# Nine more feed-forward slices as seven block products, with four single PSUM banks beside the attention's own

## The chip, the cores and the metric

The kernel runs on one core of a Trainium2 chip. The metric is the device time of one execution in microseconds (us). A run of the kernel before is a handful of executions; their median is given, and one more execution is recorded by the hardware profiler. Instructions are named by engine: PE is TensorE (matmuls), PEld its weight loads, DVE VectorE, ACT ScalarE, POOL GpSimd, SP SyncE, which issues most of the DMAs. L554 is line 554 of the kernel before.

## The reference, cut to what matters

One inference step of a two-layer decoder for 1024 prompt tokens and 8 sample tokens, which share all weights. Each layer is a mixer (layer 0: a gated linear recurrence and cross-attention into a memory; layer 1: stick-breaking attention over a shared key/value set, for the samples with pages of an old cache, and again cross-attention), and then a feed-forward network (FFN). D_MODEL is 1024, D_FF is 2816, all in float32. The change is in the FFN:

```python
def swiglu(h, w_gu, w_down):
    gate, up = jnp.split(h @ w_gu, 2, axis=-1)
    return (jax.nn.silu(gate) * up) @ w_down
...
    for l in range(DEPTH):
        ...
        h = h + rmsnorm(mix, g[1])
        h = h + rmsnorm(swiglu(rmsnorm(h, g[2]), w_gu[l], w_down[l]), g[3])
```

## The kernel before

**Tiling.** The activations lie with features on the 128 partitions and tokens on the free axis. The tokens form two groups: group 0 has 512 prompt tokens, group 1 has the other 512 and the 8 samples, 520 in all, always handled as two halves of 260 columns. To keep float32 accuracy, every operand is split into a high and a low part (`split_w` L253 for weights, `split_to` L283 for activations: a copy on ACT that rounds, a subtraction on DVE), and each product is three matmuls: high by high, high by low, low by high.

**The FFN.** The 22 slices of 128 hidden features are done in five parts of 5, 5, 4, 4 and 4 slices (`PARTS`, L615). In a part, each slice forms gate and up, their SwiGLU product is split into a tile of its own ("mid"), and then the part's down-projection (8 output blocks) adds to the result `R`. The plain form of a slice in group 1 takes 2 (gate, up) x 8 (blocks of 128 inputs) x 3 (split) x 2 (halves) = 96 matmuls of 260 columns.

**The block form.** `gate_up_w` (L526) treats a slice as a 2 x 2 block product, gate and up by upper and lower half of the inputs, times upper and lower half by the two halves of the tokens, and forms it from seven block products (Strassen, in Winograd's order): 7 x 4 x 3 = 84 matmuls. It needs four sums of weight blocks, which `weight_sums` (L590) makes ahead of time in DRAM by DMAs from DRAM to DRAM, half of them accumulating, all issued from POOL; and four sums of activation blocks for each pair of input blocks, which `sums_w` (L329) makes on DVE and ACT and puts into tiles `YT`. The products are gathered in four PSUM banks `Q(0)` to `Q(3)` (pa, pb, pc, pd at L559), with copies on ACT from one bank to the next (L561, L564) and additions on DVE (L572 to L578). Before the change only layer 1 of group 1, the last stage, uses it: `ffn_w` (L617) has 4 plain slices (`gate_up_q`, L501), in whose shade the activation sums are made, and then 18 in block form.

**PSUM.** PSUM has eight banks. Up to the last stage four of them are two double tiles `mmp`, one `mm` tile for each projection (`proj`, L269), three are single tiles `S()` for attention, transposes and the like, and one is `NS()`. For the last stage all are closed (L1439), and a pool `quads` of four tags with two buffers each takes their place; `S()` and `NS()` then take turns in two of its tags.

**Order of the work.** The program is written as generators. `weave` (L235) draws steps from several of them in given proportions; the framework's scheduler then orders each engine's instructions at compile time from that, and adds the waits. Each engine runs its own instructions in that fixed order. The stages around the change, in order (L1386 to L1443): layer 0's mixer for both groups and the FFN of group 0; then the shared keys and values of group 0; then (L1419) group 0's layer-1 attention together with parts 0 and 1 of group 1's layer-0 FFN; then (L1420) its parts 2, 3 and 4; group 1's keys and values; then (L1432) group 1's layer-1 attention and the samples' together with group 0's layer-1 FFN; and last (L1441 to L1443) group 1's layer-1 FFN in block form.

**Marks.** A step of `weight_sums` issues one DMA. So that it isn't issued too early, ACT copies one column of a recent result (`after()`) to a small tile, POOL copies that one (L605, the mark), and the DMA is queued behind the mark on POOL. The 40 steps of layer 1's sums lie in the stages of L1419 (16) and L1420 (24). POOL also issues the indirect loads of the old cache's pages (`page_loader`, L957), which the samples' attention uses in the stage of L1432: DVE multiplies a page tile (L923 for keys, L935 for values) that lies in one of the four buffers of `cpool`.

Of the kernel before, what the change touches and what calls it, by code (L numbers as in the profile page):

```python
# [9 lines left out]
F32 = mybir.dt.float32  # L10
# [8 lines left out]
P = 128  # L19
# [4 lines left out]
def tile_decoder(  # L24
# [22 lines left out]

    def pool(name, bufs, **kw):
        return ctx.enter_context(tc.tile_pool(name=name, bufs=bufs, **kw))
# [12 lines left out]
    cpool = pool("cpool", 4)  # L62
    banks = ctx.enter_context(ExitStack())
# [5 lines left out]
    uid = [0]  # L69

    def nm(s):
        uid[0] += 1
        return f"{s}_{uid[0]}"
# [10 lines left out]
    turn = [0]  # L84

# [3 lines left out]
    def NS():  # L89
        if single:  # L90
            return S()
        return nsp.tile([P, 512], F32, tag="ns", name=nm("ns"))
# [21 lines left out]
    def S():  # L114
        if single:
            turn[0] += 1
            return Q(3 * (turn[0] % 2))
# [211 lines left out]
    def sums_w(xs, ops):  # L329
# [4 lines left out]
        for k in range(4):  # L334
# [4 lines left out]
            o = (k % 2) * h  # L339

# [6 lines left out]
            for d, p, a, b in (  # L347
# [5 lines left out]
            ops.append([  # L353
                x0[:, :, :h], x1[:, :, :h], x1[:, :, h:n], z[:, :, o : o + h], u[:, :, o : o + h],
                y[:, :, :h], y[:, :, h : 2 * h],
            ])
            yield

    def YT():
        return xpool.tile([P, 2, NG[1]], F32R, tag="x0", name=nm("y"))  # L360
# [140 lines left out]
    def gate_up_q(l, f, xt):  # L501
# [3 lines left out]
        for j in range(2):  # L505
            w = split_w(w_gu[l], 0, ND, j * DFF + f * P)
            pp = [Q(2 * j + a) for a in range(2)]
            for k in range(ND):
                wh, wl = w[k]
                for wi, (wt, xi) in enumerate(((wh, 0), (wh, 1), (wl, 0))):  # L510
                    for a in range(2):
                        nc.tensor.matmul(  # L512
                            pp[a][:, :h], wt, xt[k][:, xi, a * h : (a + 1) * h],
                            start=(k == 0 and wi == 0), stop=(k == ND - 1 and wi == 2),
                        )
            for a in range(2):
# [3 lines left out]
                else:  # L520
                    last = nc.vector.tensor_mul(d, d, pp[a][:, :h])
        mt = M(F32R)
        split_to((mt[:, 0, :n], mt[:, 1, :n]), sg[:, :n])
        return mt, last

    def gate_up_w(l, f, ops, spl, raws):  # L526
# [53 lines left out]
        split_to((mt[:, 0, :n], mt[:, 1, :n]), sg[:, :n])  # L580
        return mt

    sums = {}
# [6 lines left out]
    def weight_sums(l, parts, after):  # L590

        for i in parts:
# [6 lines left out]
            for d, a, add in (  # L599
# [3 lines left out]
                tok = small([P, 1], tag="rr")  # L603
                nc.scalar.copy(tok, after())
                mark = nc.gpsimd.tensor_copy(small([P, 1], tag="mk", bufs=1), tok)  # L605
# [11 lines left out]
    class ffn_w:  # L617


        def __init__(self, l, x, plain):  # L620
            self.g, self.l, self.x, self.ops, self.plain, self.n, self.r, self.pi = 1, l, x, [], plain, 0, 0, 0
            self.R = self.acc = None
# [853 lines left out]
```

## Time and profile before

| | us |
|---|---|
| median of 3 runs | 2540.22 |
| lowest and highest of them | 2537.18, 2541.53 |
| the profiled execution | 2539.07 |
| its span, first to last instruction | 2537.4 |
| PE busy | 2503.8 |
| DVE busy | 1594.9 |
| ACT busy | 1220.6 |

The span is what the profile's views divide up; the profiled execution took 1.67 us more than its span. Busy times are unions of an engine's instructions; PE's ends are modelled, so that a full PE is better read from how many matmuls it finishes in a stretch. In a group's row stand line, engine, operation, the tile written and those read, the shapes, the count, then busy time and the mean of one in ns, and last the idle time of the engine just before these instructions and who ended it. In a view by windows each engine has its busy time and, in brackets, its number of instructions.

### The profile page before, as it was taken

The page shows a single profiled execution, that of the slowest core. Times are in us where ns is not written, and L with a number is a line of the kernel's source. Part 1 is how long each engine was busy: PE and PEld are TensorE (multiplying, and loading weights), DVE is VectorE, ACT ScalarE, POOL GpSimd, SP SyncE. Part 2 cuts the span into 40 slices and gives each one's busy share as a digit, 9 for nine tenths or more (in the row PEclk, how much of TensorE's full clock was granted, in tenths as well). Part 3 has the DMA queues.
Part 4 walks back from the last instruction along what each step waited for, and adds up shares of the span by engine and source line. Part 5 has one row for each costly group of instructions (what it writes and reads, how often), then busy time and mean ns, then how long its engine had stood idle before and what let it go on. Part 6 is the DMA issues. An engine that isn't in the chain of part 4 may idle for free. (4 is left out here: it accounts for less than half of the span.)

```text
span 2537.4 us, 40627 instructions
## 1 busy us (share of the span) xinstructions
PE 2503.8 (99%) x15437; PEld 2168.8 (85%) x15437; DVE 1594.9 (63%) x2860; ACT 1220.6 (48%) x2342; POOL 95.6 (4%) x139
## 2 busy tenths in 40 slices
PE   8999999999999999999999999999999999999998
PEld 6888888877877888989999989876676797999997
DVE  6666556655765576656544585776678638855665
ACT  6346543233434454555433454554455445554444
POOL 1000000000000000011111100012000000000000
PEclk9999999999999999999999999999999999999999
DMA  6352242234644446576678876544343333364542
GB/s 185 111 163 67 71 154 80 63 105 119 180 124 133 128 148 186 151 185 168 166 193 214 244 186 191 152 145 119 111 142 117 97 117 121 122 188 144 150 138 68
DMA packets 502221, 358.20 MB, mean 141 GB/s; under 512 B 19077, under 2 KB 451794, under 8 KB 502026
## 3 DMA queue, kind: packets, MB, share of 16 engines
q1 hardware_dynamic: 483466, 301.08, 39.8%
q0 software_dynamic: 18560, 54.53, 9.0%
q8 instruction: 121, 1.98, 0.3%
q14 instruction: 74, 0.61, 0.1%
HBM read 325.73 MB, written 75.94 MB: 158 GB/s over the span
## 5 line engine op out<-in xcount | busy, mean ns | idle before, releaser
L277 PE MATMUL mm<-x,ws 128*128 128x260 f32 (+1 forms) x7968 | 1425.2, 335 | 0.8 <-ACT x L401 0.8
L277 PEld LDWEIGHTS mm<-x,ws 128*128 128x128 f32 x7968 | 1190.5, 188 | 175.0 <-issue 28.5
L263 ACT CAST ws<-w 128x512 fp32r<-128x512 f32 x728 | 430.4, 592 | 724.7 <-PE mm L277 590.5
L264 DVE TENSOR_TENSOR ws<-w,ws 128x512 fp32r<-128x512 f32 x728 | 474.1, 654 | 301.2 <-ACT ws L263 290.7
L277 PE MATMUL mm<-m,ws 128*128 128x512 f32 (+1 forms) x2112 | 415.2, 347 | 0.0
L277 PEld LDWEIGHTS mm<-m,ws 128*128 128x128 f32 x2112 | 327.3, 189 | 53.5 <-issue 7.1
L669 PE MATMUL q<-m,ws 128*128 128x260 f32 x1056 | 128.8, 283 | 0.0
L669 PEld LDWEIGHTS q<-m,ws 128*128 128x128 f32 x1056 | 127.2, 188 | 0.4 <-ACT hT L487 0.2
L545 DVE TENSOR_TENSOR ws<-w,ws 128x512 fp32r<-128x512 f32 x126 | 86.4, 691 | 60.1 <-ACT ws L544 55.3
L554 PE MATMUL q<-y,ws 128*128 128x260 f32 x864 | 112.9, 283 | 0.0
L544 ACT CAST ws<-w 128x512 fp32r<-128x512 f32 x126 | 77.9, 621 | 69.0 <-PE q L669 26.1
L554 PEld LDWEIGHTS q<-y,ws 128*128 128x128 f32 x864 | 107.6, 188 | 0.0
L449 DVE TENSOR_TENSOR r<-r,mm 128x512 f32<-128x512 f32 (+1 forms) x96 | 66.1, 688 | 65.0 <-PE mm L277 64.1
L294 DVE TENSOR_SCALAR t<-mm 128x512 f32<-128x512 f32 (+1 forms) x82 | 56.8, 692 | 72.2 <-PE mm L277 71.2
L705 DVE TENSOR_TENSOR t<-t,mm 128x512 f32<-128x512 f32 (+1 forms) x66 | 45.6, 690 | 87.7 <-PE mm L277 87.7
L554 PE MATMUL q<-x,ws 128*128 128x260 f32 x648 | 86.3, 282 | 0.0
L298 DVE TENSOR_TENSOR t<-t,t 128x512 f32<-128x512 f32 (+1 forms) x66 | 45.8, 693 | 60.3 <-ACT t L297 60.2
L554 PEld LDWEIGHTS q<-x,ws 128*128 128x128 f32 x648 | 81.3, 188 | 0.0
L317 DVE TENSOR_TENSOR st<-st,n 128x512 f32<-128x512 f32 (+1 forms) x98 | 67.1, 692 | 6.7 <-ACT n L316 5.0
L285 DVE TENSOR_TENSOR m<-t,m 128x512 fp32r<-128x512 f32 (+1 forms) x88 | 61.1, 694 | 2.8 <-ACT m L284 1.4
L284 ACT CAST m<-t 128x512 fp32r<-128x512 f32 (+1 forms) x88 | 54.8, 623 | 11.7 <-DVE t L705 2.4
L964 POOL DMA_INDIRECT c<-in_cache_sb_k,pidx x16 | 16.4, 1025 | 1015.4 <-DVE x L285 796.7
(337 smaller groups left out, 2556.6 us busy)
## 6 DMA issues: line engine op xcount, KB each, us to landing
w<-in_w_gu SPq DMA_DIRECT2D x334, 256.0 KB
w<-in_w_down SPq DMA_DIRECT2D x160, 256.0 KB
w<-in_w_in_a SPq DMA_DIRECT2D x80, 256.0 KB
wsum<-in_w_gu POOLq DMA_DIRECT2D x18, 1024.0 KB, 9.2
w<-wsum SPq DMA_DIRECT2D x72, 256.0 KB
w<-in_w_o SPq DMA_DIRECT2D x64, 256.0 KB
wsum<-in_w_gu POOLq DMA_DIRECT2D x12, 1280.0 KB, 10.8
w<-in_w_mem_kv SPq DMA_DIRECT2D x32, 256.0 KB
```

The costliest lines, as they stand in the source:

```text
L263: nc.scalar.copy(ws[:, 0, :n, :], raw[:, :n, :])
L264: nc.vector.tensor_sub(ws[:, 1, :n, :], raw[:, :n, :], ws[:, 0, :n, :].bitcast(F32))
L277: nc.tensor.matmul(ps[:, a, : PW[g]], wt, xt[k][:, xi, o : o + PW[g]], start=(k == 0 and wi == 0), stop=(k == nk - 1 and wi == 2),)
L284: nc.scalar.copy(dst[0], src)
L285: nc.vector.tensor_sub(dst[1], src, dst[0].bitcast(F32))
L294: nc.vector.tensor_scalar(sv(x, g), pv(ps, g), -44.0, None, op0=ALU.max)
L317: nc.vector.tensor_add(acc[:, :n], acc[:, :n], t[:, :n])
L449: nc.vector.tensor_add(dst, dst, pv(ps, g))
L544: nc.scalar.copy(w[:, 0, :], src)
L545: nc.vector.tensor_sub(w[:, 1, :], src, w[:, 0, :].bitcast(F32))
L554: nc.tensor.matmul(ps[:, :h], w[:, wj, k * P : (k + 1) * P], x[:, xi, :], start=(first and k == 0 and wi == 0), stop=(k == 3 and wi == 2), ...
L669: nc.tensor.matmul(pp[a][:, :h], wt, mids[k][:, xi, a * h : (a + 1) * h], start=(k == 0 and wi == 0), stop=(k == nf - 1 and wi == 2),)
```

## The change

Group 1's layer-0 FFN is handed over after part 1: parts 2 to 4 (12 slices) become an `ffn_w` with three plain slices and nine in block form, which goes on adding to the same `R`. For it the two double tiles `mmp` are closed and a pool `quads` with one buffer for each of its four tags takes their four banks; after part 4 `mmp` comes back. `S()` and `NS()` keep their own banks to the end, so in the last stage too the four `Q` banks have one buffer each, where they had two, and `S()` no longer uses them. `sums_w` now yields after each activation sum (16 steps), and `gate_up_q` draws 5, 6 and 5 of them between its matmuls in three plain slices; thus the last stage has three plain slices, not four, and 19 in block form. In layer 0 the activation sums lie in `apool` tiles.

Layer 0's weight sums for parts 2 to 4 (24 DMAs) are new and are woven into group 1's mixer and group 0's FFN. Of layer 1's 40, 16 stay beside parts 0 and 1, 8 stay beside parts 2 to 4, and 16 move to the stage of the last attention. The mark on POOL now reads the recent result itself (`now[0]`), without ACT's copy. The attention in the stage of L1419 gets the share 28 in place of 24.

```diff
-    mmp = banks.enter_context(tc.tile_pool(name="mmp", bufs=2, space=PSUM))
-    smp = banks.enter_context(tc.tile_pool(name="smp", bufs=3, space=PSUM))
-    nsp = banks.enter_context(tc.tile_pool(name="nsp", bufs=1, space=PSUM))
+    mmp = None
     single = []
...
+    def set_banks(one):
+
+        nonlocal mmp
+        banks.close()
+        single.clear()
+        if one:
+            single.append(banks.enter_context(tc.tile_pool(name=nm("quads"), bufs=1, space=PSUM)))
+        else:
+            mmp = banks.enter_context(tc.tile_pool(name=nm("mmp"), bufs=2, space=PSUM))
...
     def S():
-        if single:
-            turn[0] += 1
-            return Q(3 * (turn[0] % 2))
         return smp.tile([P, 512], F32, tag="s", name=nm("s"))
...
-    def gate_up_q(l, f, xt):
+    def gate_up_q(l, f, xt, side, n_side):
...
-                        nc.tensor.matmul(
+                        ins = nc.tensor.matmul(
                             pp[a][:, :h], wt, xt[k][:, xi, a * h : (a + 1) * h],
                             start=(k == 0 and wi == 0), stop=(k == ND - 1 and wi == 2),
                         )
+                c = j * ND + k + 1
+                for _ in range(c * n_side // 16 - (c - 1) * n_side // 16):
+                    with tc.issue_after(ins.ins):
+                        next(side, None)
...
-                tok = small([P, 1], tag="rr")
-                nc.scalar.copy(tok, after())
-                mark = nc.gpsimd.tensor_copy(small([P, 1], tag="mk", bufs=1), tok)
+                mark = nc.gpsimd.tensor_copy(small([P, 1], tag="mk", bufs=1), now[0])
...
         def spl(self):
             self.n += 1
-            if self.pi and self.n % 8 in (1, 4, 6):
+            if (self.pi or not self.rows) and self.n % 8 in (1, 4, 6):
                 return cpool.tile([P, 2, 512], F32R, tag="c", name=nm("ws"))
...
         def raws(self):
             self.r += 1
-            if self.pi and self.r % 2:
+            if not self.rows and self.r % 2:
+                return B().rearrange("p (k m) -> p k m", k=4)
+            if self.rows and self.pi and self.r % 2:
...
-    weave((a0.mem(), 8), (a1.fq(), 8))
+    w0 = weight_sums(0, range(2, 5))
+    weave((a0.mem(), 8), (a1.fq(), 8), (islice(w0, 6), 7))
...
-    weave((o0.finish(), 17), (chain(a1.v(), a1.qm(A)), 8))
+    weave((o0.finish(), 17), (chain(a1.v(), a1.qm(A)), 8), (islice(w0, 6), 7))
     f0 = ffn(0, 0, o0.x)
-    weave((a1.core(), 22), (f0.part(0), 9))
+    weave((a1.core(), 22), (f0.part(0), 9), (islice(w0, 8), 9))
     a1.open()
-    weave((a1.sample(), 6), (a1.gate(), 4), (f0.part(1), 9))
+    weave((a1.sample(), 6), (a1.gate(), 4), (f0.part(1), 9), (w0, 5))
...
-    ws = weight_sums(1, range(5), lambda: f1.now)
-    weave((chain(b0.sb(), b0.mem()), 24), (chain(f1.part(0), f1.part(1)), 18), (islice(ws, 16), 17))
-    weave((chain(f1.part(2), f1.part(3), f1.part(4)), 24), (ws, 24))
+    ws = weight_sums(1, range(5))
+    weave((chain(b0.sb(), b0.mem()), 28), (chain(f1.part(0), f1.part(1)), 18), (islice(ws, 16), 17))
+    set_banks(True)
+    fw = ffn_w(0, o1.x, (5, 6, 5), 2, False, f1.R)
+    weave((chain(fw.part(2), fw.part(3), fw.part(4)), 24), (islice(ws, 8), 8))
+    f1.acc = fw.acc
+    set_banks(False)
...
-        (chain(f0.part(0), f0.part(1), f0.part(2), f0.part(3)), 34),
+        (chain(f0.part(0), f0.part(1), f0.part(2), f0.part(3)), 34), (ws, 17),
     )
...
-    banks.close()
-    single.append(ctx.enter_context(tc.tile_pool(name="quads", bufs=2, space=PSUM)))
-    f1 = ffn_w(1, o1.x, 4)
+    set_banks(True)
+    f1 = ffn_w(1, o1.x, (5, 6, 5), 0, True)
```

More of the change, by code (lines that the diff above doesn't have):

```diff
@@ L648, in part @@
                 if f0 + j < self.plain:
-                    mt, ins = gate_up_q(l, f0 + j, self.x)
-                    mids.append(mt)
-                    with tc.issue_after(ins.ins):
-                        for _ in range((1, 2, 1, 0)[j]):
-                            next(self.sums, None)
+                    mids.append(gate_up_q(l, f0 + j, self.x, self.sums, self.steps[j]))
+                    now[0] = mids[-1][:, 0, 0:1].bitcast(F32)
                 else:
@@ L1002, in heads2 @@
             evac(out[-1][:, h % 2, :], ps, g)
+            now[0] = out[-1][:, h % 2, 0:1]
             yield
```

55 lines of the change are left out of this document (31 added, 24 removed).

## The prediction

> **What bounds the kernel now.** I began with the page's busy times and then cut the span into stages with the view by windows. Its columns are the stretch, its length, then PE, PEld, DVE, ACT and POOL busy (with instruction counts), the clock, the DMA share and GB/s.
>
> ```profile
> span 2537.4 us, 40627 instructions
> ## 1 busy us (share of the span) xinstructions
> PE 2503.8 (99%) x15437; PEld 2168.8 (85%) x15437; DVE 1594.9 (63%) x2860; ACT 1220.6 (48%) x2342; POOL 95.6 (4%) x139
> ```
>
> ```profile
> core 0: us, PE busy (x) PEld busy (x) DVE busy (x) ACT busy (x) POOL busy (x), PEclk, DMA share, GB/s
> 1030.00:1260.00 230.00, 227.84 (x1671) 211.38 (x1671) 130.91 (x262) 120.94 (x263) 22.53 (x34) 1.00 0.67 169
> 1260.00:1458.00 198.00, 198.00 (x1651) 197.75 (x1650) 97.52 (x143) 80.13 (x146) 29.67 (x45) 1.00 0.83 215
> 1605.00:1830.00 225.00, 219.31 (x912) 158.59 (x911) 149.22 (x255) 114.21 (x218) 28.21 (x24) 0.99 0.45 132
> 1830.00:2045.00 215.00, 213.44 (x904) 154.00 (x904) 154.48 (x257) 106.19 (x211) 0.00 (x0) 1.00 0.38 113
> 2155.00:2202.00 47.00, 46.93 (x387) 46.48 (x388) 44.42 (x96) 23.43 (x48) 0.00 (x0) 1.00 0.32 90
> 2202.00:2521.00 319.00, 318.99 (x2662) 317.96 (x2661) 181.62 (x341) 166.41 (x338) 0.00 (x0) 1.00 0.48 141
> ```
>
> PE is the bound throughout. The stage that the change rewrites (1260 to 1458: parts 2 to 4 of layer 0's feed-forward network, second half) has no idle PE at all, at full clock: 198.00 us for 1651 matmuls, 119.9 ns each. The stage that already works by block products (2202 to 2521) runs at the same pace, 318.99 / 2662 = 119.8 ns. So a matmul taken out of either is worth 0.12 us, as long as nothing new stops PE. The stages with the attention have the idle PE: 2.2 us in 1030 to 1260, 5.7 us in 1605 to 1830.
>
> **Step 1, matmuls removed.** The groups of PE, shapes kept apart, give the counts:
>
> ```profile
> L554 PE MATMUL q<-y,ws 128*128 128x260 f32 x864 | 112.9, 283 | 0.0
> L554 PE MATMUL q<-x,ws 128*128 128x260 f32 x648 | 86.3, 282 | 0.0
> ...
> L512 PE MATMUL q<-x,ws 128*128 128x260 f32 x384 | 46.7, 283 | 1.8 <-DVE r L449 1.8
> ```
>
> L512 has 384 matmuls for 4 plain slices: 96 each. L554 has 864 + 648 = 1512 for 18 block slices: 84 each. Layer 0 turns nine slices over, and layer 1 has three plain slices where it had four, so ten slices lose 12 matmuls: 120 x 119.8 ns = **-14.4 us**. All ten lie on PE's path. The Trainium skill (TensorE: Matmul & The Clock Gate, section Back-to-back issue gap) gives N / 2.4 + 2.5 ns at full clock, 110.8 ns for 260 columns; by that the term would be -13.3 us. The two rows above disagree with it by 9 ns, and I keep them.
>
> **Step 2, what a block slice adds on DVE, ACT and SP.** Seven weight splits instead of four:
>
> ```profile
> L545 DVE TENSOR_TENSOR ws<-w,ws 128x512 fp32r<-128x512 f32 x126 | 86.4, 691 | 60.1 <-ACT ws L544 55.3
> ...
> L544 ACT CAST ws<-w 128x512 fp32r<-128x512 f32 x126 | 77.9, 621 | 69.0 <-PE q L669 26.1
> ```
>
> DVE has 7 x 0.69 + 4 x 0.42 (four half-width operations, L572 to L578; 0.42 is L577's row in step 4) + 0.69 (L285, full width again) = 7.2 us per slice beside 84 x 0.12 = 10.1 us of PE. ACT, with 7 x 0.62 and six short ones, is about as busy. SP issues seven loads of 256 KB instead of four, 27 more in this stage. Its DMA share is 0.83 with 24 weight-sum transfers in it; the block stage without them has 0.48. With eight left, a third of the difference, I get 0.48 + 0.12 = 0.60. PE hides all this: **0**. If that cover went, DVE would have to pass 10.1 us per slice, 2.9 more than it has.
>
> **Step 3, the two further changes of banks.** The double banks are closed and opened twice more. The one change of banks in the trace shows a gap on PE:
>
> ```profile
> 2155.07 2.03 PE L512 MATMUL q<-x,ws 128*128 128x260 f32 x15 [1.75 <-DVE r L449]
> ```
>
> PE waited 1.75 us for the last down-projection's evacuation. Two more such: between 0 and +3.5. It is 0 where the first single banks are those whose double tile was emptied a round earlier, and then the old 1.75 may go too, so the lower end is -1.75. The fw stage's last tile uses banks q2 and q3, which favours 0 at its end. I take **+1.0**.
>
> **Step 4, four single banks with one buffer each (layer 1 had two).** Inside a slice the order of products leaves each bank empty at least one product (1.4 us) before it is written again. The tight place is the start of each down-projection, whose second half writes q1, the bank of the last product:
>
> ```profile
> 2299.31 8.90 PE L669 MATMUL q<-m,ws 128*128 128x260 f32 x73
> ...
> 2299.51 0.42 DVE L577 TENSOR_TENSOR t<-t,q 128x260 f32<-128x260 f32 x1
> ```
>
> L577 reads that bank until 2299.93. With one buffer the first matmul into q1 waits for it, 0.62 us after the down-projection's first; all behind it on PE waits too. Eight such starts (five parts of layer 1, three of layer 0): at most 8 x 0.62 = +5.0. At least 0, if the compiler puts the first half's matmuls ahead: with four mids, three are ready, 9 matmuls or 1.1 us. That instructions are put out of the written order is seen on POOL, where the last attention's first page load stands before the first mark of the weight sums, though it is written after it:
>
> ```profile
> 809.33 1.19 POOL L964 DMA_INDIRECT c<-in_cache_sb_k,pidx  x1 [796.68 <-DVE x L285]
> ...
> 1044.07 0.68 POOL L605 COPY mk<-rr 128x1 f32<-128x1 f32 x1 [227.79 <-ACT rr L604]
> ```
>
> So I lean to the low end: **+1.0**.
>
> **Step 5, the operands of the blocks.** Per use they cost 48 half-width DVE operations, 48 x 0.42 = 20 us. In layer 0 they lie in three slices (288 x 0.12 = 34.5 us of PE) with 12 weight splits (8.3) and three evacuations (3 x 1.5, two half and one full operation): 33 us of DVE. That just fits, and the last operand is first used at the seventh product, 8.6 us later: 0. In layer 1 the same must now be done in three slices instead of four while the previous feed-forward network finishes; there the window 2155 to 2202 has DVE at 44.42 of 47.
>
> ```profile
> 2197.13 0.43 DVE L285 TENSOR_TENSOR y<-b,y 128x260 fp32r<-128x260 f32 x1
> ```
>
> ```profile
> L554 PE MATMUL q<-x,ws x648: 277/282/363, 2203.6 to 2493.5; 128*128 128x260 f32 x162
> ```
>
> The last operand is ready at 2197.6, 6.0 us before the first block product and 14.6 before its own. The start moves 11.5 us forward, and DVE is rid of the fourth slice's four splits and evacuation ahead of it, 4.3 us: the slack falls by 7.2, to some 7 for the last operand, but to 1 or 2 for those of the second and third products, which start only 1.4 and 2.9 us after the first. Between 0 and +3 (two products): **+0.5**.
>
> **Step 6, weight sums moved.** 24 new DRAM-to-DRAM sums for layer 0 go into the stages ahead of 1030 us, and 16 of layer 1's 40 go to the last attention's stage. Their marks no longer pass over ACT: 40 copies less there, off the path; in turn a late POOL holds the tile that a mark reads, which is written again only a part later (over 30 us): 0. Layer 0's are there long before their use, and the 1260 to 1458 window shows 24 of them beside full PE: 0 (up to +1 for the state loads that they slow down). The denser attention in 1030 to 1260, 24 steps in 24/28 of the stage, had 2.2 us of idle PE: 0 (up to +1). The last attention's stage is the sore place. Each mark makes POOL wait for a result of the stage around it, and the page loads and the next sum stand behind it; the page loads share POOL's DMA queue with the sums as well:
>
> ```profile
> L608 POOL DMA_DIRECT2D wsum<-in_w_gu x20: 998/1028/1093, 1071.7 to 1476.6; - x20
> ...
> DMA to landing us min/median/max: 9.0/10.3/13.2
> ```
>
> ```profile
> L964 POOL DMA_INDIRECT c<-in_cache_sb_v,pidx x16: 950/985/3727, 1691.5 to 1773.1; - x16
> ...
>   DVE c L935: 4.0, 3
> ...
> DMA to landing us min/median/max: 3.4/3.8/6.8
> ```
>
> ```profile
> 1771.39 1.44 POOL L964 DMA_INDIRECT c<-in_cache_sb_v,pidx  x1 [12.99 <-PE ns L937]
> 1773.13 0.95 POOL L964 DMA_INDIRECT c<-in_cache_sb_v,pidx  x1 [0.30 <-issue]
> ```
>
> ```profile
> 1776.81 1.23 DVE L935 TENSOR_TENSOR c<-c,sc 128x1024 f32<-128x1024 f32 x1 [2.75 <-DMA c<-in_cache_sb_v,pidx]
> ```
>
> ```profile
> 1778.69 0.51 PE L1306 MATMUL s<-b,trir 128*128 128x512 f32 x1 [1.65 <-DVE b L285]
> ```
>
> The last value pages are used as they land: DVE waited 2.75 us, the attention's split (L285) stood behind it on DVE, and PE lost 1.65. Three value loads are that tight (L935 waited three times, 4.0 us). Sixteen sums over 1605 to 2045 come every 26 us; one takes 10.3, so a load meets one about 4 times in 10 and waits half of it, 5 us: 3 x 0.4 x 5 = 6 us of DVE, of which PE lost 1.65 / 2.75 = 0.6. That is 3.6 at even odds, 0 at best, and 3 x 10.3 x 0.6 = 18.5 at worst; as some loads are issued while POOL stands at a mark with nothing in its queue, I take **+2.5**.
>
> **Sum.** -14.4 + 1.0 + 1.0 + 0.5 + 2.5 = -9.4. The profiled execution took 2539.07 (span 2537.4 and 1.7 around it): 2529.7. The median of 2540.22 is 1.15 above that execution, so I say **2531**.
>
> **The rivals.**
> *Nothing is lost (0.20).* Steps 3 to 6 are hidden and the old bank change goes with them: 2540.2 - 14.4 - 1.75 = 2524. For it: no idle PE from 2202 to 2521. Against it: steps 3 and 6 show PE waiting for exactly such things.
> *Single banks (0.15).* Steps 3 and 4 at their upper ends, 3.5 + 5.0, with 0.5 + 2.5: -2.9, so 2537, no change that counts. For it: L577 ends after the down-projection's second matmul. Against it: the reordering.
> *Page loads (0.13), the slower side.* At step 6's worst, the three tight loads each wait for a whole sum: -14.4 + 2.5 + 18.5 = +6.6, 2547. It decides from 17 us of PE loss, 28 us of DVE waiting for pages, where the profile has 4. For it: one queue and no lead. Against it: a sum occupies the queue 10 us in 26, and all three loads would have to meet one. The Trainium skill (DMA: Bandwidth & Descriptors, section SWDGE vs HWDGE vs iDMA) says that only one queue is allocated for DMAs issued from GpSimd, which speaks for this rival; no row here shows a page load behind a sum.
> *The blocks don't pay (0.05).* Late operands or weight blocks stretch the ten slices to their old 11.5 us: 2540. Against it: 18 slices at 119.8 ns.
> The forecast itself, 2526 to 2535: 0.47.
>
> About 0.2% (5 us) is what a measurement of this kernel can tell from no change. Faster by more: 0.47 + 0.20 = 0.67; within: 0.15 + 0.05 = 0.20; slower: 0.13. The range 2523 to 2543 leaves out the page-load rival and little else.
>
> **What would show it.** L554 at 28 x 84 = 2352 matmuls, L512 at 6 x 96 = 576. A PE gap before the first L512 of each change of banks (step 3), after each last L554 (step 4), before the first L554 (step 5), and at L1306 behind DVE's L923 or L935 between 1600 and 1830 (step 6). I am wrong if layer 0's twelve slices and three down-projections take more than 198 - 13 + 3 = 188 us, or if idle PE in the last attention's stage grows by more than 6 us.

## The result, and the profile after

| | before | after |
|---|---|---|
| median (lowest to highest of 4 runs each), us | 2540.31 (2537.18 to 2541.53) | 2641.49 (2640.26 to 2648.99) |
| profiled execution, its span, us | 2539.07, 2537.4 | 2641.61, 2639.9 |
| idle PE: span less PE busy, us | 33.6 | 116.0 |
| ACT busy, us | 1220.6 | 1392.3 |
| ACT table loads | 4 | 129 |

The ratio is 1.041 [1.0397, 1.0422]: 101 us slower, far outside the range of the prediction. In the kernel after, most lines have moved down: L277 is now L281, L554 is L559, L512 is L513, L1269 is L1283, L1306 is L1320, L661 is L672.

The page of the kernel after, its head and three of its groups:

```profile
span 2639.9 us, 40841 instructions
## 1 busy us (share of the span) xinstructions
PE 2523.9 (96%) x15317; PEld 2170.5 (82%) x15317; DVE 1621.1 (61%) x2969; ACT 1392.3 (53%) x2492; POOL 120.5 (5%) x187
...
L559 PE MATMUL q<-x,ws 128*128 128x260 f32 x1008 | 134.3, 282 | 0.0
...
L559 PE MATMUL q<-y,ws 128*128 128x260 f32 x912 | 119.5, 283 | 0.2 <-ACT q L566 0.2
...
L1320 PE MATMUL s<-b,trir 128*128 128x512 f32 (+3 forms) x96 | 41.1, 428 | 44.4 <-ACT b L288 42.3
```

The 120 matmuls are gone (15437 to 15317), and the block products still run without idle PE ahead of them. The last row says where time went: 44.4 us of idle PE ahead of the attention's matmul into `s` (before, L1306), and it is ACT that ended it. The view by windows (columns as in the prediction) says in which stage:

```profile
1030.00:1260.00 230.00, 225.75 (x1648) 209.09 (x1648) 139.44 (x291) 121.05 (x253) 19.25 (x32) 1.00 0.65 164
1260.00:1458.00 198.00, 197.10 (x1621) 195.88 (x1620) 120.20 (x229) 92.13 (x179) 18.13 (x24) 0.99 0.72 197
1603.00:2050.00 447.00, 376.46 (x1450) 264.42 (x1449) 256.29 (x426) 312.05 (x448) 45.87 (x52) 0.95 0.49 139
```

The last of these windows in the kernel before:

```profile
1603.00:2050.00 447.00, 439.75 (x1874) 319.59 (x1873) 306.96 (x517) 222.56 (x434) 28.21 (x24) 1.00 0.41 123
```

The stage that was rewritten (second row) is nearly full. The last attention's stage (third row), whose PE work the change does not touch, has 70.5 us of idle PE where it had 7.25, ACT is busier there than DVE, and the granted clock is 0.95 instead of 1.00. From the first to the last score matmul of group 1's attention, this stage took 341.8 us before (1612.0 to 1953.8) and 426.0 after (1611.1 to 2037.1). What ACT does there stands in its groups from 1600 to 2100:

```profile
L1283 ACT ACT_TABLE_LOAD x33 | 42.3, 1283 | 0.6
L1328 ACT ACT_TABLE_LOAD x21 | 26.9, 1283 | 0.4
L300 ACT ACT_TABLE_LOAD x18 | 23.1, 1283 | 0.3
```

ACT loads a set of function tables again and again. In its timeline (start, duration; idle time before in brackets) one sees how, first in the kernel after, then at the same place before:

```profile
1612.53 0.32 ACT L1282 ACTIVATE b<-b 128x128 f32<-128x128 f32 x1
1612.87 1.28 ACT L1283 ACT_TABLE_LOAD   x1
1614.17 0.31 ACT L1283 ACTIVATE b<-b 128x128 f32<-128x128 f32 x1
1615.16 0.30 ACT L288 CAST b<-b 128x128 fp32r<-128x128 f32 x1 [0.68 <-DVE b L1287]
```

```profile
1613.43 0.32 ACT L1268 ACTIVATE b<-b 128x128 f32<-128x128 f32 x1
1613.78 0.31 ACT L1269 ACTIVATE b<-b 128x128 f32<-128x128 f32 x1
```

The exponential (L1282) and the logarithm behind it (L1283) stood 0.03 us apart; now a load of 1.28 us stands between them. PE's timeline of the kernel after has the matmul that waits for the result:

```profile
1615.51 0.33 PE L1320 MATMUL s<-b,trir 128*128 128x128 f32 x1 [1.29 <-ACT b L288]
```

PE lost 1.29 us, one load, and before the change nothing at this place. Exp and Ln can share one set, and up to here they do. The change puts Silu into layer 0's block stage, in the middle of the program; Silu needs another set, and the load that should bring the common set back (L672) is written into the last part's down-projection without any dependency. The trace has no load at that line; tied behind the last Silu (experiment 1) one is there. From this I infer that in the compiled order it stood ahead of the Silus, where the common set was still in and there was nothing to load. The first load after the start is at L524 (1264.4 us, for Silu), and from 1464.0 us on each change from Ln to Exp or back is a load: 129 x 1.283 = 165.5 us of ACT, where the 4 of before were 5.1. The Trainium skill (ScalarE: Activation LUTs, section Table sets: the hidden batching unit) counts one load for Ln and then Exp, since one set holds both; the rows differ, as after a Silu each of the two brought a load. Why the common set was not loaded there no run shows. The same page's section What ACT_TABLE_LOAD costs gives 2.66 us for a switch, 1.38 of it a drain; here L1282's end and L1283's start are 1.32 us apart, so that no drain is seen beside the load.

### The profile page after: what moved, and what is told of

It is laid out like the page before. It is cut to its first block, busy times and chain, and to the rows that moved or that the text cites. A ratio compares the mean times of both kernels' runs of the same rounds, so it can differ in the third digit from the quotient of the medians.

```text
span 2639.9 us, 40841 instructions
## 1 busy us (share of the span) xinstructions
PE 2523.9 (96%) x15317; PEld 2170.5 (82%) x15317; DVE 1621.1 (61%) x2969; ACT 1392.3 (53%) x2492; POOL 120.5 (5%) x187
## 5 line engine op out<-in xcount | busy, mean ns | idle before, releaser
L281 PE MATMUL mm<-x,ws 128*128 128x260 f32 (+1 forms) x6816 | 1302.9, 346 | 7.4 <-DVE ws L268 1.7
L281 PEld LDWEIGHTS mm<-x,ws 128*128 128x128 f32 x6816 | 1061.3, 190 | 187.9 <-issue 31.4
L267 ACT CAST ws<-w 128x512 fp32r<-128x512 f32 (+1 forms) x688 | 405.0, 590 | 571.3 <-PE mm L281 426.0
L268 DVE TENSOR_TENSOR ws<-w,ws 128x512 fp32r<-128x512 f32 (+1 forms) x688 | 446.4, 653 | 281.7 <-ACT ws L267 267.0
L281 PE MATMUL mm<-m,ws 128*128 128x512 f32 (+1 forms) x1536 | 346.4, 373 | 0.3 <-DVE m L289 0.3
L281 PEld LDWEIGHTS mm<-m,ws 128*128 128x128 f32 x1536 | 259.2, 191 | 55.1 <-issue 7.3
L680 PE MATMUL q<-m,ws 128*128 128x260 f32 x1632 | 200.2, 283 | 0.0
L680 PEld LDWEIGHTS q<-m,ws 128*128 128x128 f32 x1632 | 196.7, 188 | 1.4 <-DVE t L582 0.5
L550 DVE TENSOR_TENSOR ws<-w,ws 128x512 fp32r<-128x512 f32 x164 | 112.5, 691 | 81.5 <-ACT ws L549 78.8
L549 ACT CAST ws<-w 128x512 fp32r<-128x512 f32 x164 | 101.7, 622 | 98.5 <-PE q L680 33.9
L559 PE MATMUL q<-x,ws 128*128 128x260 f32 x1008 | 134.3, 282 | 0.0
L559 PEld LDWEIGHTS q<-x,ws 128*128 128x128 f32 x1008 | 126.4, 188 | 0.0
L559 PE MATMUL q<-y,ws 128*128 128x260 f32 x912 | 119.5, 283 | 0.2 <-ACT q L566 0.2
L559 PEld LDWEIGHTS q<-y,ws 128*128 128x128 f32 x912 | 113.6, 188 | 0.5 <-ACT q L566 0.4
L1320 PE MATMUL s<-b,trir 128*128 128x512 f32 (+3 forms) x96 | 41.1, 428 | 44.4 <-ACT b L288 42.3
L513 PE MATMUL q<-x,ws 128*128 128x260 f32 x576 | 74.4, 291 | 6.3 <-DVE r L450 4.6
L513 PEld LDWEIGHTS q<-x,ws 128*128 128x128 f32 x576 | 72.6, 196 | 8.0 <-issue 3.8
L450 DVE TENSOR_TENSOR r<-r,mm 128x512 f32<-128x512 f32 (+1 forms) x72 | 49.4, 687 | 38.1 <-PE mm L281 37.0
L1320 PEld LDWEIGHTS s<-b,trir 128*128 128x128 f32 x96 | 19.0, 198 | 65.2 <-ACT b L288 56.7
```

The lines of the kernel that those rows point to most:

```text
L267: nc.scalar.copy(ws[:, 0, :n, :], raw[:, :n, :])
L268: nc.vector.tensor_sub(ws[:, 1, :n, :], raw[:, :n, :], ws[:, 0, :n, :].bitcast(F32))
L281: nc.tensor.matmul(ps[:, a, : PW[g]], wt, xt[k][:, xi, o : o + PW[g]], start=(k == 0 and wi == 0), stop=(k == nk - 1 and wi == 2),)
L450: nc.vector.tensor_add(dst, dst, pv(ps, g))
L513: ins = nc.tensor.matmul(pp[a][:, :h], wt, xt[k][:, xi, a * h : (a + 1) * h], start=(k == 0 and wi == 0), stop=(k == ND - 1 and wi == 2),)
L549: nc.scalar.copy(w[:, 0, :], src)
```

## The experiments

Two theories for the 101 us: *tables*, that the loads cost nearly all of it; and *sums*, that the weight sums moved beside the last attention's page loads (the prediction's slower rival) hold up DVE and PE, with the tables on a side path. Each experiment was timed against the kernel before on the same chip. "After" is the kernel after. All of them compute the same function.

**1. The load tied behind the last Silu.** After, with

```diff
-        nc.scalar.activation(sg[:, h:n], gt[:, :h], AF.Silu)
+        silu_w[0] = nc.scalar.activation(sg[:, h:n], gt[:, :h], AF.Silu)
...
-                nc.scalar.preload_act_table_set("natural_log_exp_and_others")
+                with tc.issue_after(silu_w[0].ins):
+                    nc.scalar.preload_act_table_set("natural_log_exp_and_others")
```

> The changed kernel; the one difference is that the load of the table set with both Exp and Ln is queued on ACT behind layer 0's last Silu (and layer 1's behind its own). Tables theory (125 of the 129 ACT table loads, 1.28 us each, are what slows the last attention's stage): about 5 loads are left and the time falls by some 105 us to 2525 to 2540, with the table-free sum of the prediction, 2531, in the middle. Rival (the 16 weight sums moved into the last attention's stage delay its page loads and marks): the loads go, but the stage stays over 60 us longer than before, over 2600. Rival (single banks, bank changes): no gain from this edit, as PE's waits for them remain, 2630 or more.

2550.57 us, ratio 1.0052 [1.0038, 1.0066], with 5 table loads. The tables were (1.041 - 1.0052) x 2540 = 91 us of the 101. The time is above the 2525 to 2540 that were expected: the kernel is still slower than before, by 13 us, so something else eats the 14.4 us of matmuls and 13 more. By windows:

```profile
1605.00:1830.00 225.00, 208.29 (x818) 148.26 (x817) 142.89 (x244) 108.01 (x204) 40.39 (x40) 0.97 0.55 153
1830.00:2045.00 215.00, 209.12 (x852) 149.16 (x851) 153.93 (x258) 105.20 (x208) 11.71 (x16) 0.99 0.55 153
```

The two windows that had 7.25 us of idle PE before have 22.6 here, and in the first the clock is 0.97.

**2. One Silu in the kernel before.** Before, with one line behind the stage of L1420, whose result nobody reads:

```diff
+    nc.scalar.activation(small([P, 1], tag="rr"), f1.now, AF.Silu)
```

> The kernel before, with one Silu of one column (its result unused) on ACT after group 1's layer-0 feed-forward network, and no load of the common set behind it. No sums moved, no banks changed, no blocks added. Tables theory: Exp and Ln alternate from there to the last stage as in the changed kernel, about 129 loads, and the time rises by 90 to 125 us to 2630 to 2665. Rivals (moved sums; single banks): nothing that they name is in it, 2538 to 2545.

2631.7 us, ratio 1.0365 [1.0349, 1.0381]: one Silu of 128 numbers costs 94 us. Its groups on ACT in 1600 to 2100 (L1269 and L1314 of before are L1283 and L1328 of after):

```profile
L1269 ACT ACT_TABLE_LOAD x33 | 42.3, 1283 | 0.6
L1314 ACT ACT_TABLE_LOAD x21 | 26.9, 1283 | 0.4
```

They are the loads of after, count for count (129 in all here too). With blocks, single banks and sums all as before, the tables alone do nearly all that the change did, 94 of 101 us.

**3 and 4. The sixteen sums put back beside the block slices**, 3 with the tables as in after, 4 with them as in experiment 1:

```diff
-    weave((chain(fw.part(2), fw.part(3), fw.part(4)), 24), (islice(ws, 8), 8))
+    weave((chain(fw.part(2), fw.part(3), fw.part(4)), 24), (ws, 24))
...
-        (chain(f0.part(0), f0.part(1), f0.part(2), f0.part(3)), 34), (ws, 17),
+        (chain(f0.part(0), f0.part(1), f0.part(2), f0.part(3)), 34),
```

> The changed kernel with the 16 weight sums taken out of the last attention's stage and put back beside layer 0's parts 2 to 4 (24 there, as before); the tables are left as the change has them. Tables theory: still 129 loads, 2630 to 2645. Rival (moved sums and page loads): the last attention's stage gets back most of its 95 us, 2540 to 2560.

> Both edits: the common table set behind the last Silu, and the 16 sums back beside layer 0's parts 2 to 4. Against the first kernel of this call it gives step 6 of the prediction alone. If step 6's estimate of +2.5 us for page loads behind sums holds, this one is 1 to 5 us faster than that one; if the sums cost nothing there, they are equal within 1.5 us; if 24 sums beside the blocks starve their weights, it is slower by 2 us or more.

3: 2647.22, ratio 1.0431 [1.0415, 1.0447]. 4: 2547.71, ratio 1.0037 [1.0023, 1.0051]. The first falls to *tables*, 2 us above its range: without a sum beside the last attention the loss is still there, 110 us. The second is 2.9 us faster than experiment 1, as expected for a step 6 of +2.5, but it says less than it seems to, for it moved a cost. Idle PE in 1605 to 2045 fell from 22.6 to 6.0 us, and in 1260 to 1480 it rose from 0.9 to 14.7. The sums now compete with the block slices' weight loads; the view of waits of experiment 4, 1260 to 1530 (total us, times, longest):

```profile
ACT ws L549 <- DMA w<-wsum: 20.0, 3, 8.2
...
ACT ws L267 <- DMA w<-in_w_down: 10.4, 2, 8.4
```

ACT waited up to 8.4 us for a weight, and PE stopped at the down-projections for 4.92, 2.55 and 3.91 us. So the sums cost time in either place, and the next runs look for one where they don't.

**5. The sums spread over earlier stages.** Experiment 1, with layer 1's sums divided: 9 beside group 0's FFN parts 2 to 4, 6 in the stages of keys and values, 17 beside the attention of L1419, 8 beside the blocks, none beside the last attention:

```diff
-    weave((chain(a1.merge(), a1.mem()), 12), (a1.mem_sample(), 20), (chain(f0.part(2), f0.part(3)), 16))
-    drain(f0.part(4))
+    ws = weight_sums(1, range(5))
+    weave((chain(a1.merge(), a1.mem()), 12), (a1.mem_sample(), 20), (chain(f0.part(2), f0.part(3)), 16), (islice(ws, 4), 4))
+    weave((f0.part(4), 8), (islice(ws, 5), 5))
...
-    drain(kv_proj(0, xk0))
+    weave((kv_proj(0, xk0), 8), (islice(ws, 3), 3))
...
-    weave((b0.heads(), 8), (o1.finish(), 17))
+    weave((b0.heads(), 8), (o1.finish(), 17), (islice(ws, 3), 3))
```

> The first experiment's kernel (common table set behind the last Silu), with 32 of layer 1's 40 weight sums in the stages before layer 0's block slices (15 of them ahead of the layer-1 attention of group 0, 17 beside it), 8 beside the block slices, and none in the last attention's stage. Theory (in the first experiment's kernel the 16 sums in the last attention's stage cost PE some 16 us there, and in the fourth's the 24 beside the blocks starve their weight loads by some 21 us): neither is left, 2526 to 2535, faster than before. Rival (the last attention's stage is slow for another reason, the changed banks or order): it stays at 2545 to 2552. Rival (the early stages have no room either): 2535 to 2545, with idle PE between 660 and 1030 us, where before has none.

2539.77, ratio 1.0003 [0.9994, 1.0012] over 12 runs: equal to before, where experiment 1 was 13 us slower. This is the time of the second rival, for which the early stages have no room either. The last attention is as long as it was (342.1 us). But the stage that holds the six sums among the keys and values has 8.4 us more of idle PE. The window there, in experiment 5 and in before:

```profile
940.00:1050.00 110.00, 101.29 (x498) 82.12 (x496) 62.98 (x109) 46.78 (x85) 8.29 (x12) 0.98 0.85 237
```

```profile
940.00:1050.00 110.00, 109.64 (x595) 91.77 (x594) 65.44 (x116) 51.21 (x96) 1.32 (x2) 1.00 0.57 175
```

PE finishes 97 matmuls less, with the DMA share at 0.85 instead of 0.57.

**6 to 8. Three parts of experiment 5 alone.** 6 makes layer 0's twelve slices plain, in the single banks, 108 matmuls more (`ffn_w(0, o1.x, (0,) * 12, ...)`, and the preload behind the plain form's Silu); layer 0's weight sums are still made, for no use. 7 starts layer 0's plain slices in the other two banks:

```diff
-            pp = [Q(2 * j + a) for a in range(2)]
+            pp = [Q((2 * j + a) ^ (0 if l else 2)) for a in range(2)]
```

8 adds, beside the last attention, 16 marks on POOL without a sum behind them:

```diff
+    def bare_marks(n):
+        for _ in range(n):
+            nc.gpsimd.tensor_copy(small([P, 1], tag="mk", bufs=1), now[0])
+            yield
```

> As the spread-sums kernel, but layer 0's twelve slices of parts 2 to 4 are all plain in the four single banks: no block products and no activation sums there, the weight sums of layer 0 still made and unused. It takes 108 matmuls of 260 columns back. Theory (a matmul removed there is worth 0.12 us, step 1): 12.0 to 14.5 us slower than the spread-sums kernel. Rival (the blocks stretch their slices, so that they are worth little): within 6 us of it.

> As the spread-sums kernel, but layer 0's plain slices write banks q2 and q3 for the gate and q0 and q1 for the up. Theory (step 3: PE's 2.7 us gap at the first change of banks is a wait for the double tile that lies in the first two banks): the gap before the first single-bank matmul goes to under 0.5 us, and the time falls by 1.5 to 3 us. Rival (all four banks become free together when the pool is closed): the gap stays over 2 us and the times agree within 1.5 us.

> As the spread-sums kernel, with 16 bare marks on POOL in the last attention's stage, where the change has its marks, but no sum behind them. If the marks (POOL standing at one while page loads are behind it) are what costs there, it is 6 us or more slower than the spread-sums kernel. If it is the sums' transfers themselves, it agrees with it within 2.5 us.

6: 2553.6, ratio 1.0062 [1.005, 1.0075], so nine slices in blocks are worth 2553.6 - 2539.77 = 13.8 us. 7: 2538.12, ratio 0.9996 [0.9987, 1.0004]; PE's gap at the first change of banks is 1.01 us in both, so it does not matter which banks come first (the gap of over 2 us that both theories started from was not there in experiment 5 either). 8: 2539.38, ratio 1.0006 [0.9997, 1.0014]: marks alone cost nothing; what cost time in experiment 1 were the transfers.

**9. All sums ahead of the keys and values.** Experiment 1, with both layers' sums in one chain: 44 ahead of 885 us, 12 beside the attention of L1419, 8 beside the blocks.

```diff
+    ws = chain(weight_sums(0, range(2, 5)), weight_sums(1, range(5)))
...
-    weave((a1.core(), 22), (f0.part(0), 9), (islice(w0, 8), 9))
+    weave((a1.core(), 22), (f0.part(0), 9), (islice(ws, 12), 13))
```

> Common table set behind the last Silu; all 64 weight sums in one row: 44 before 885 us (6, 6, 12, 9, 8 and 3 in the stages of the mixer and of group 0's layer-0 network), none in the stages of keys and values and of the heads, 12 beside group 0's layer-1 attention, 8 beside the block slices, none in the last attention's stage. Theory (what the spread-sums kernel lost, some 9 us between 941 and 1044 us, are transposes, evacuations and first loads delayed by the sums there): 2525 to 2534, faster than before by 5 to 13 us. Rival (the sums cost PE about the same wherever they stand): 2536 to 2545.

2541.5, ratio 1.0015 [1.0006, 1.0024]. A miss. The window of 660 to 805 us, then the same of before:

```profile
660.00:805.00 145.00, 140.18 (x592) 104.60 (x591) 98.81 (x151) 57.52 (x111) 11.70 (x16) 1.00 0.79 215
```

```profile
660.00:805.00 145.00, 145.00 (x621) 109.76 (x620) 102.02 (x156) 59.07 (x115) 0.00 (x0) 1.00 0.50 150
```

With the DMA share at 0.79 instead of 0.50 this stage finishes 29 matmuls less. DVE's waits in 600 to 830 us name two loads, neither a weight's:

```profile
DVE c L938 <- DMA b<-qd: 9.8, 2, 6.1
DVE c L950 <- DMA c<-in_cache_mem_v: 9.0, 4, 3.4
```

Before, the same two waits were 2.1 and 5.9 us. These are the loads of the samples' attention into the memory, again just in time. ACT also waited for weights, 8.1 us for `w<-in_w_gu`, where before it did not, so that the weights' loads came late too.

**10 and 11. Eight sums, beside the page loads or behind them.** Both have 32 of layer 1's sums earlier, and eight in the last attention's stage; 10 in its first half, with the page loads, 11 in its second:

```diff
-        (chain(f0.part(0), f0.part(1), f0.part(2), f0.part(3)), 34), (ws, 17),
+        (chain(f0.part(0), f0.part(1), f0.part(2), f0.part(3)), 34), (chain(pause(9), ws), 17),
```

> As the kernel with no sums beside keys, but 8 of layer 1's sums, taken from the early stages, stand in the first half of the last attention's stage, between the page loads. Theory (the sums hurt there most because page loads stand behind them in POOL's DMA queue, beside what they take from SP's loads): 8 to 13 us slower than that kernel, with DVE waiting for page loads some 6 us. Rival (a sum costs about the same in the whole stage, through the 16 DMA engines): 3 to 6 us slower, like the next.

> As the kernel before this one, but the 8 sums stand in the second half of the last attention's stage, where the page loads are over and the samples' loads come from SP's queue. Theory (POOL's DMA queue shared with the page loads is the larger part): 2 to 6 us slower than the kernel without sums in that stage, and 4 or more faster than the one with 8 beside the page loads. Rival (contention on the DMA engines alone): equal to the latter within 2 us.

10: 2552.28, ratio 1.0054 [1.0041, 1.0067]. 11: 2536.24, ratio 0.9996 [0.9987, 1.0004]. The same eight sums in the same stage: 16 us between the medians (9.1 between the spans of the profiled executions). 10 came out as its theory said, 10.8 us slower than experiment 9. 11 is 16.0 us faster than 10, but also 5.3 faster than experiment 9, where 2 to 6 slower were expected: in 9 these eight sums stand in the early stages. The windows of 10, then of 11:

```profile
1605.00:1830.00 225.00, 208.95 (x835) 149.32 (x834) 141.68 (x239) 108.34 (x205) 40.39 (x40) 0.97 0.55 157
1830.00:2045.00 215.00, 213.60 (x879) 152.74 (x878) 156.85 (x264) 107.15 (x212) 0.00 (x0) 1.00 0.41 120
```

```profile
1605.00:1830.00 225.00, 217.42 (x889) 156.05 (x888) 150.19 (x259) 113.93 (x220) 28.45 (x24) 0.99 0.42 128
1830.00:2045.00 215.00, 210.63 (x879) 151.73 (x877) 152.37 (x252) 104.67 (x206) 11.84 (x16) 0.99 0.55 152
```

The half with the sums loses idle PE in both (POOL's count tells which), but the first half, with the pages, loses 8.5 us more of it in 10 than in 11, and 54 matmuls of progress; the second loses 3.0 in 11. The queue that sums and page loads share is only part of the 8.5: PE's gaps behind a page load are 5.49 and 1.00 us in 10 and 1.45 in 11, and another 4.02 in 10 stand behind a weight load that SP issued, for which PE has no gap in 11.

**12. Smaller sums, put where nothing waits.** Experiment 1, with the sums taken over the slices in block form alone (the six plain ones left out of the transfers, the count of 64 unchanged), 39 of them ahead of 885 us (but none in 660 to 805 us, where experiment 9 had lost), 17 beside the attention of L1419 and 8 beside the blocks, none among the keys and values or beside the last attention; and with layer 0's activation sums queued on DVE behind the last evacuation of part 1:

```diff
-            nc.vector.tensor_add(dst, dst, pv(ps, g))
+            evac_at[0] = nc.vector.tensor_add(dst, dst, pv(ps, g))
...
-                    with tc.issue_after(ins.ins):
+                    with tc.issue_after((ins if l else evac_at[0]).ins):
...
+    FIRST = {0: 13, 1: 3}
...
+            nf -= max(0, FIRST[l] - f0)
+            f0 = max(f0, FIRST[l])
...
-    weave((a1.core(), 22), (f0.part(0), 9), (islice(w0, 8), 9))
+    weave((a1.core(), 22), (f0.part(0), 9), (islice(ws, 13), 14))
...
-    drain(f0.part(4))
+    weave((f0.part(4), 8), (islice(ws, 5), 6))
```

> Common table set behind the last Silu; weight sums only for the slices that are done as blocks (the three plain slices' are left out of two of the eight parts: 8 of the 64 transfers move 256 KB and 8 move 512 KB, in place of 1 MB and 1.25 MB); none beside the samples' loads, keys, heads or page loads (8, 7, 13, 6 and 5 before 885 us, 17 beside group 0's layer-1 attention, 8 beside the block slices); and layer 0's activation sums queued on DVE behind the last evacuation of part 1. Theory (blocks win 13 us in layer 0, and what the other kernels lost again are sums beside loads that something waits for, and 2 us at the change of banks): 2524 to 2532, faster than before by 6 us or more, with under 1 us of idle PE at the change of banks. Rival (64 sums cost about the same anywhere): 2536 to 2542.

2529.72 (2527.13 to 2531.31) against 2538.86 for before: ratio 0.996 [0.9946, 0.9974], 9 us faster, the only version that beats the kernel before. Its windows:

```profile
660.00:805.00 145.00, 145.00 (x620) 109.69 (x620) 102.27 (x157) 59.48 (x115) 0.00 (x0) 1.00 0.49 150
...
1605.00:1830.00 225.00, 217.49 (x869) 154.84 (x869) 150.89 (x262) 113.67 (x219) 28.50 (x24) 0.98 0.41 123
1830.00:2045.00 215.00, 214.02 (x931) 156.30 (x931) 152.53 (x250) 106.44 (x208) 0.00 (x0) 1.00 0.37 113
```

660 to 805 is full again, because no sum runs there, and the last attention's stage has the idle PE of before within 1.3 us. The profiled span is 7.8 us shorter than before: -14.4 for the matmuls, +6.4 of idle PE up to 2520 us (28.7 less 22.3). That its 9.1 us are near the prediction's sum (-9.4) is a coincidence, for that sum was made for another kernel. Three things were changed at once; what part of the gain is due to the smaller sums, to their places and to the order on DVE was not taken apart.

## Why the prediction was wrong, step by step

The failed step is **step 2**, and in it the sentence on ACT: "with 7 x 0.62 and six short ones, is about as busy ... PE hides all this: 0". It counted how long ACT's new instructions run and not which functions they are. Until the change Silu stood only at the end of the program; the one that the change puts into its middle brought 125 table loads, +91 us (experiment 1), +94 by itself (experiment 2). ACT is not busy enough for this to bound it (312 of 447 us); each load lies in the chain Exp, Ln, split, matmul of the attention, where PE waits. The signs were in the profile of before. These are ACT's groups there:

```profile
L519 ACT ACT_TABLE_LOAD x1 | 1.3, 1283 | 0.0
L758 ACT ACT_TABLE_LOAD x1 | 1.3, 1283 | 1.3 <-PE q L756 1.3
L759 ACT ACT_TABLE_LOAD x1 | 1.3, 1283 | 0.0
```

There the Silu of the last stage loads its set (L519), and behind it the Ln of L758 and the Exp of L759, two lines in succession, each load one; no load stands at L661, so the preload there was already without effect. It cost two loads at the end of the program; a reader who asks what follows a Silu would have seen what the same Silu does ahead of an attention that alternates Exp and Ln.

This is also where one of the prediction's two signs of being wrong did show: idle PE in the last attention's stage grew by 63 us, and 6 was the limit.

**Step 6 was mis-sized, and its mechanism was the smaller part.** I took +2.5, from 0 to 18.5. With the tables out of the way (experiment 1) idle PE in 1605 to 2045 grew by 22.6 - 7.25 = 15.3 us, near the upper end. But that end was worked out from page loads, and they are not most of it. Source L979 of experiment 1, the issues of the value pages, with who waited and the landing times:

```profile
L979 POOL DMA_INDIRECT c<-in_cache_sb_v,pidx x16: 946/995/3752, 1686.6 to 1778.8; - x16
...
  DVE c L950: 7.9, 3
...
DMA to landing us min/median/max: 3.3/4.4/10.1
```

Before, these were 4.0 us for three waits and at most 6.8 to landing; the page-load rival needed 28 us of such waits. POOL's, DVE's and PE's timelines of experiment 1 show one case whole:

```profile
1755.48 1.14 POOL L614 DMA_DIRECT2D wsum<-in_w_gu  x1
1756.92 1.05 POOL L979 DMA_INDIRECT c<-in_cache_sb_v,pidx  x1 [0.31 <-issue]
1758.27 0.97 POOL L979 DMA_INDIRECT c<-in_cache_sb_v,pidx  x1 [0.30 <-issue]
```

```profile
1765.72 1.23 DVE L950 TENSOR_TENSOR c<-c,sc 128x1024 f32<-128x1024 f32 x1 [5.55 <-DMA c<-in_cache_sb_v,pidx]
1766.86 0.68 DVE L1327 TENSOR_TENSOR b<-b,s 128x512 f32<-128x512 f32 x1
```

```profile
1767.59 0.79 PE L1322 MATMUL s<-b,cmpr 128*128 128x512 f32 x1 [5.25 <-DVE b L1327]
```

A sum is issued, two page loads right behind it; DVE waits 5.55 us for the page with the attention's own operation (L1327) queued behind, and PE 5.25 for that. With one gap of 0.95 this is all that PE lost behind page loads: 6.2 us, before 1.9. The larger losses stand behind loads that SP issues, in another queue than the sums, the samples' queries and a weight:

```profile
1683.74 1.23 DVE L938 TENSOR_TENSOR c<-c,b 128x1024 f32<-128x1024 f32 x1 [4.81 <-DMA b<-qd]
1690.25 0.79 PE L1322 MATMUL s<-b,trir 128*128 128x512 f32 x1 [3.76 <-ACT b L288]
...
1711.71 0.62 ACT L267 CAST ws<-w 128x512 fp32r<-128x512 f32 x1 [4.43 <-DMA w<-in_w_gu]
1712.58 0.48 PE L1322 MATMUL s<-b,trir 128*128 128x128 f32 x1 [4.32 <-ACT b L288]
```

Query loads cost PE 9.2 us in four gaps (before 3.7 in two), this weight 4.32 and a load of the cached memory (`c<-in_cache_mem_v`) 2.08 (before nothing). So the step failed in pricing the three value loads alone: of some 16 us of growth they are 4.3, and loads outside POOL's queue are 12. It also took even odds that a sum is in the queue, while in the case above POOL issues the sum as soon as its mark is free and the pages follow 1.4 us behind; and sixteen sums over 440 us come every 27.5 us, not 26, which changes little. "Off the path" for the marks themselves holds (experiment 8). The early sums, "0 (up to +1)", held for layer 0's 24: up to 1050 us PE idles 11.8 us in the kernel after and 11.1 before. They did not with layer 1's beside them: experiment 5 idles 8.4 us more in 940 to 1050, experiment 9 4.8 us more in 660 to 805. The denser attention held: of the 4.25 us of idle PE in 1030 to 1260 (before 2.16), 3.12 stand at the change of banks.

**Step 1 was right.** 13.8 us measured for nine slices, where 108 x 0.1198 = 12.9 was the reckoning. The formula cited in step 1 from the Trainium skill (TensorE: Matmul & The Clock Gate, section Back-to-back issue gap) is given there for a single isolated matmul and not for a stream of them, so the 9 ns are no disagreement about this case.

**Step 2's other half held with eight sums**: no gap of over 0.2 us ahead of a block product, and L559 still 282 ns each. The DMA share was 0.72, where I had reckoned 0.60. With 24 sums in the stage it fails (experiment 4): the share is 0.93, and it is the weights' loads that come late, with DVE waiting behind them (busy 110 of 198 us).

**Step 3 was too low, and its reason was wrong.** By PE's timeline the two new changes of banks cost 3.12 and 0.90 us in the kernel after, and the old one 1.49 instead of 1.75: +3.8, where I said +1.0 and at most 3.5. Which bank comes first is indifferent (experiment 7), as it would be if the banks come free together, with the last evacuation. In the kernel after, DVE's timeline at the first change shows what stands ahead of it:

```profile
1256.41 0.76 DVE L289 TENSOR_TENSOR a<-b,a 128x260 fp32r<-128x260 f32 x2
1257.09 1.10 DVE L351 TENSOR_TENSOR b<-x 128x260 f32<-128x260 f32 x3
1258.11 0.69 DVE L450 TENSOR_TENSOR r<-r,mm 128x520 f32<-128x520 f32 x1
```

The new activation sums (L351, L289) run first, and L450 empties the bank after them. With the order turned (experiment 12) the gap is 1.42 us, and it is 1.42 in experiment 6, which has no activation sums there; but it was 1.01 in experiment 5 with the order unturned. Only part of it is explained by this.

**Step 4: the low end, 0.** In the kernel after and in experiment 1 there is no gap over 0.2 us between a part's last block product and the down-projection. **Step 5:** two waits for weights at the plain slices in experiment 1, 0.9 us together, and none at the first block; I had said 0.5.

**The test was set wrongly too.** "Over 188 us for layer 0's twelve slices" came from a window of 198 us that held 1651 matmuls, while the work is 12 x 96 + 3 x 192 = 1728 of them, 207 us at 119.8 ns. After, 1620 matmuls took 1258.95 to 1455.6, 196.7 us, where 1620 x 0.1198 = 194: near what the blocks should give, and my own test would have called it a failure.

**The sum again**, for the profiled execution of experiment 1: span 2547.8 - 2537.4 = +10.4. Matmuls -14.4; idle PE in all windows up to 2520 us, 41.9 less 22.3 = +19.6 (15.3 of it in the last attention's stage); that leaves +5.2, and the mean granted clock was 0.994 against 0.996, about 5 us of 2540. For the kernel after, idle PE is +82.4 and the clock 0.986, some 25 us: -14.4 + 82.4 + 25 = 93 of 102.5. The 9 that are left, and what part of the clock's share is due to the waits, are not settled.

## What to carry to other kernels

When a change moves an ACT function to another place, ask which function set is in before and after it, and look for table loads behind the same function in the old profile; a preload that depends on nothing may be put where it does nothing, so queue it behind the instruction that made it necessary. A transfer from DRAM to DRAM is not free because its result is early: place it where no load lands just in time, in its own queue or in another, and expect that moving it trades one such place for another. When two changes of a kernel are suspected, take out the larger one first and then test the rest against the kernel before, for the smaller one is invisible beside it.

## What the runs showed of the hardware

- A table load took 1283 ns wherever it stood. Where the function behind it waited for nothing else, it began 0.02 us later (L1283 at 1614.17).
- In the last attention's stage the granted clock was lower where PE idled more. In 100 us of it, first before and then after:

```profile
1700.00:1800.00 100.00, 95.14 (x369) 65.92 (x369) 70.91 (x120) 51.66 (x98) 17.82 (x14) 0.98 0.44 128
```

```profile
1700.00:1800.00 100.00, 79.87 (x290) 55.29 (x289) 59.98 (x102) 67.15 (x102) 20.58 (x20) 0.91 0.57 154
```

  PE busy 80% has a clock of 0.91, where 95% had 0.98. Experiment 10 against 11 goes the same way: 0.97 and 0.99 in 1605 to 1830 us, about 4.5 us beside the 8.5 of idle PE. There a wait may cost more than its own length, but it is no rule that these runs show: in the kernel before the clock was 1.00 in 0 to 100 us with PE busy 90.14, and 0.98 in 500 to 600 us with PE busy 99.99.
- Landing of a page load: a median of 3.8 us and at most 6.8 in the kernel before, up to 10.1 in experiment 1, with sums in the same queue. Loads of SP's queue were late there too: in experiment 1 the three longest gaps of PE behind them were 4.32, 3.76 and 3.30 us.
